# A third summed pair in the gate and up projections of an encoder block

## The chip, the cores and the metric

The kernel runs on one core of a Trainium2 chip. The metric is the device time of one execution in microseconds (us). One core has a matrix engine (TensorE, PE in the profile; its weight loads are listed as PEld), VectorE (DVE), ScalarE (ACT), GpSimd (POOL) and SyncE (SP, which here only issues DMAs). TensorE writes to PSUM, the other engines read PSUM and SBUF. All engines run side by side and wait for each other by semaphores; each takes its own instructions strictly in the order of its own list.

## The reference

One encoder layer over 256 tokens of width 2048, all in fp32: attention in two kinds of heads, cross-attention into 256 memory tokens, and a gated feed-forward network, each with a residual, and a last normalization. The change touches the feed-forward network:

```
hf = rms_norm(x, g_ffn)                                    # 256 x 2048
x  = x + (silu(hf @ w_gate) * (hf @ w_up)) @ w_down        # w_gate, w_up: 2048 x 5632, w_down: 5632 x 2048
out = rms_norm(x, g_final)
```

with `silu(z) = z * sigmoid(z)`.

## The kernel before

**Precision.** Every fp32 operand of a product is split into a high part (a cast to the reduced fp32r format) and a low part (what the cast left over). `split_into` (line 97) does it: ScalarE casts (line 99), VectorE subtracts (line 100). `mm` (line 89) then issues three matmuls: high x high (line 91), high x low (92), low x high (93). So each block product is three matmuls of 128 x 128 stationary by 128 x 512 moving columns. The activations are the stationary side and are split once; the weights are the moving side, come from HBM as fp32, are used once per core, and have to be split on the way.

**The weight path.** SyncE issues a DMA of 1 MB into one of three raw tiles (`wraw`, 128 x 2048). ScalarE and VectorE split it, 1024 columns at a time, into pairs of tiles `wh`, `wl`, a ring of four. Raw tile, ring tile and PSUM bank are each given out again when their last reader is done, so a DMA waits for VectorE, a cast waits for PE, and PE waits for VectorE.

**Wide projections.** The feed-forward network handles 512 hidden columns in a narrow first chunk (`narrow_chunk`, line 799) and 1024 in each of five wide chunks (`wide_chunk`, line 817). A wide chunk is a gate projection, an up projection (both `wide_result`, line 729), the product with the activation function, and the transposition of the result for the down projection (`wide_add`, line 749). All three go through `wide_project` (line 680). Its unit is a *pair*: two blocks of 128 along the contracted dimension, two token blocks, two blocks of 512 output columns. A pair of kind P, plain, is 2 x 2 x 2 = 8 block products, 24 matmuls. A pair of kind W uses sums of blocks (the Winograd form of Strassen's scheme): 7 block products, 21 matmuls. For that, the activations are kept as eight sums and blocks (`summed_pair`, line 663), and the weights are summed on VectorE before they are split (lines 707, 711 and 712). Three of the four output blocks share intermediate products, which collect in four PSUM banks `q1`, `q5`, `q7`, `q6` over all W pairs of a projection; after the last W pair, `leave` (line 733) takes them out with one copy on ScalarE and four operations on VectorE. The plain parts collect in four other banks, and `join` (line 742) adds the two at the end of the projection.

`GU_KINDS` (line 39) gives the kinds of the eight pairs of a gate or up projection: two of eight are W. The weights are laid out in HBM by these kinds. Within a W pair, seven blocks of weights are needed: three raw ones and four sums. Before, three split tiles of the ring take the raw blocks and two of the sums, and the other two sums go into a tile pair of their own (`wh2`, `wl2`).

**The activation function.** After a gate projection ScalarE computes a sigmoid of the four result blocks (line 824) and VectorE multiplies it with the result (line 825). The narrow chunk does the same with a scale (lines 808, 809).

**What sets the order.** The order of DMA issues is the program's (`keep_in_program_order`). The order of each engine's other instructions is set by the framework's planner, which runs the program against its own estimate of times and takes what is ready; so splits for a later pair stand between the matmuls and the joins of an earlier one. `pacc` and `pps` hold four PSUM banks each: the plain sums of the next projection can begin only when the joins have emptied the banks of the last.

Of the kernel before, what the change touches and what calls it, by code (L numbers as in the profile page):

```python
# [19 lines left out]
P = 128  # L20
S = 256
# [17 lines left out]
GU_KINDS = "PPWPWPPP"  # L39
# [35 lines left out]
def encoder_block(ctx: ExitStack, tc: tile.TileContext, a, out):  # L75
# [3 lines left out]
    wp = ctx.enter_context(tc.tile_pool(name="wp", bufs=3))  # L79
# [4 lines left out]
    pps = ctx.enter_context(tc.tile_pool(name="pps", bufs=4, space=PS))  # L84
    tables = ExitStack()
# [26 lines left out]

    def weights(src, fine=False, pool=None, before_k=None, cut=None, raw=None):
# [6 lines left out]
        if not begun:  # L120
            raw = wp.tile([P, 2048], F32, name="wraw", tag="wraw", bufs=3)
# [10 lines left out]
        for k in range(0, nk, step):  # L132
            n = min(step, nk - k)
            if pool:
                w = pool((P, n, ncols), "w")
            else:
                w = [wp.tile([P, 1024], F32R, name=x, tag=x, bufs=4)[:, :n * ncols].rearrange("p (k c) -> p k c", k=n)
                     for x in ("wh", "wl")]
                w = Split(*w)
# [26 lines left out]
    def nat(name):  # L166
        return sb.tile([P, 512], F32, name=name, tag="nat", bufs=7)
# [19 lines left out]
    lat_raw = wp.tile([P, 2048], F32, name="wraw", tag="wraw", bufs=3)  # L187
# [14 lines left out]
    posi = const.tile([P, NT], I32, name="posi")  # L202
    invf = const.tile([P, NF], F32, name="invf")
# [62 lines left out]
    posf = const.tile([P, NT], F32, name="posf")  # L266
# [81 lines left out]
    cosr = const.tile([P, NT, 2, DR // 2], F32, name="cosr")  # L348
    sinr = const.tile([P, NT, 2, DR // 2], F32, name="sinr")
    cosd = const.tile([P, NT, 2, DD // 2], F32, name="cosd")  # L350
    sind = const.tile([P, NT, 2, DD // 2], F32, name="sind")
# [155 lines left out]
    gdb = const.tile([P, DV], F32, name="gdb")  # L507
# [126 lines left out]
    wsum = ctx.enter_context(tc.tile_pool(name="wsum", bufs=1))  # L634


    def pair_raw(src):
        raw = wp.tile([P, 2048], F32, name="wraw", tag="wraw", bufs=3)
        raw = raw.rearrange("p (b c) -> p b c", b=4)
        tc.keep_in_program_order(nc.sync.dma_start(out=raw, in_=src))  # L640
        return raw

    def w_tile(n=2, pool=None):

        pool, tags, bufs = (wp, ("wh", "wl"), 4) if pool is None else (pool, ("wh2", "wl2"), 1)
# [3 lines left out]
    def split_blocks(src, pool=None):  # L649
        w = w_tile(src.shape[1], pool)  # L650
        split_into(w, src)
        return w
# [353 lines left out]
```

## Time and profile before

| what | value |
|---|---|
| time, median of 3 runs | 1158.89 us (1158.38 to 1160.23) |
| the profiled execution's own time | 1158.9 us |
| its span, first to last instruction | 1157.1 us |
| granted TensorE clock, mean | 0.999 |
| busy: PE, DVE, ACT, POOL | 99%, 78%, 53%, 6% of the span |
| matmuls and transposes | 5510 |
| DMA | 222.13 MB, 192 GB/s on average |

Busy times are sums over the span; an engine that is busy is not always the one that others wait for. In the groups of instructions, a line gives engine, operation, output and inputs, shapes and count, then the busy time of all, the mean of one in nanoseconds, and the idle time of that engine just ahead of them with the releaser. In the waits, the three numbers are the time in all, how often, and the longest. In the timeline, a line gives the start, the time from the first start to the last end of the merged instructions, and what they are. Matmul ends are modelled, so the distance from start to start is what to read there. In the windows, each engine's busy time stands with the number of its instructions.

### The profile page before, as it was taken

To read this page: it belongs to the slowest core of one execution; us is meant where nothing else is said; L and a number is where in the kernel's file an instruction comes from. 1 tells how busy PE (TensorE), PEld (TensorE's weight loads), DVE (VectorE), ACT (ScalarE), POOL (GpSimd) and SP (SyncE) were. 2 spreads that over 40 slices of the span, in tenths; PEclk is the share of its full clock that TensorE was granted. 3 is DMA by queue.
4 is the path that set the end of the run, shared out by engine and by line. 5 is a ranking of instruction groups with operands and counts; after the bars stand their busy time and mean duration, and the time that the engine had idled before them with its cause. 6 is when DMAs were issued, how large, how long until landed. Compare 5 with 4: busy or idle time off the path is not lost.

```text
span 1157.1 us, 14401 instructions
## 1 busy us (share of the span) xinstructions
PE 1148.1 (99%) x5510; PEld 961.7 (83%) x5510; DVE 901.3 (78%) x1197; ACT 611.0 (53%) x863; POOL 69.3 (6%) x81
## 2 busy tenths in 40 slices
PE   9999999999999999999999999999999999999997
PEld 7888888888888888888888888888888888888887
DVE  7698766586867776978888787797888788798873
ACT  6755454554665565655444554564544554554552
POOL 4920000001000000000000000000000000000021
PEclk9999999999999999999999999999999999999999
DMA  9565344435755445465565555645556555555651
GB/s 356 215 218 189 113 145 168 161 146 206 272 212 182 146 149 187 174 218 182 185 214 184 206 184 192 218 181 183 202 179 223 204 181 202 192 220 202 210 204 73
DMA packets 33764, 222.13 MB, mean 192 GB/s; under 512 B 4128, under 2 KB 4896, under 8 KB 8992
## 3 DMA queue, kind: packets, MB, share of 16 engines
q1 hardware_dynamic: 32256, 216.86, 52.4%
q0 software_dynamic: 864, 3.15, 0.7%
q10 hardware_dynamic: 576, 1.21, 0.3%
q8 instruction: 43, 0.70, 0.2%
q14 instruction: 25, 0.20, 0.1%
HBM read 219.11 MB, written 2.10 MB: 191 GB/s over the span
## 4 chain that ended last, share of the span: by engine, by line
PE 98%; DMA 1%; issue 0%; DVE 0%; SPq 0%; ACT 0%; POOLq 0%; POOL 0%; DVEq 0%; ACTq 0%
PE acc L92 28%; PE acc L91 28%; PE acc L93 28%; PE q L91 2%; PE q L92 2%; PE q L93 2%; PE pt L315 2%; PE ppt L462 1%; DMA wraw<-in_w_in_lat 1%; PE psc L93 1%; PE psc L91 1%; PE psc L92 1%; PE pt L838 0%; PE acckv L93 0%; PE acckv L92 0%
## 5 line engine op out<-in xcount | busy, mean ns | idle before, releaser
L99 ACT CAST wh<-wraw 128x1024 fp32r<-128x1024 f32 (+2 forms) x399 | 399.2, 1013 | 383.1 <-PE acc L93 346.7
L100 DVE TENSOR_TENSOR wl<-wraw,wh 128x1024 fp32r<-128x1024 f32 (+2 forms) x399 | 469.0, 1184 | 166.3 <-ACT wh L99 164.4
L92 PE MATMUL acc<-wl,x2n_h 128*128 128x512 f32 x480 | 185.5, 390 | 0.0
L93 PE MATMUL acc<-wh,x2n_l 128*128 128x512 f32 x480 | 185.2, 389 | 0.0
L91 PE MATMUL acc<-wh,x2n_h 128*128 128x512 f32 x480 | 160.3, 390 | 0.0
L93 PEld LDWEIGHTS acc<-wh,x2n_l 128*128 128x128 f32 x480 | 90.1, 188 | 18.8
L91 PEld LDWEIGHTS acc<-wh,x2n_h 128*128 128x128 f32 x480 | 90.1, 188 | 18.8
L92 PEld LDWEIGHTS acc<-wl,x2n_h 128*128 128x128 f32 x480 | 90.1, 188 | 18.7
L92 PE MATMUL acc<-wl,hT_h 128*128 128x512 f32 (+1 forms) x272 | 103.7, 381 | 0.0
L93 PE MATMUL acc<-wh,hT_l 128*128 128x512 f32 (+1 forms) x272 | 103.5, 381 | 0.0
L91 PE MATMUL acc<-wh,hT_h 128*128 128x512 f32 (+1 forms) x272 | 89.4, 382 | 0.0
L92 PE MATMUL acc<-wl,x0T_h 128*128 128x512 f32 x224 | 88.2, 395 | 0.0
L93 PE MATMUL acc<-wh,x0T_l 128*128 128x512 f32 x224 | 87.8, 393 | 0.0
L91 PE MATMUL acc<-wh,x0T_h 128*128 128x512 f32 x224 | 87.4, 396 | 0.3 <-ACT x0T_h L102 0.3
L99 ACT CAST wh<-tsum 128x1024 fp32r<-128x1024 f32 x56 | 58.3, 1047 | 42.2 <-DVE tsum L712 30.8
L100 DVE TENSOR_TENSOR wl<-tsum,wh 128x1024 fp32r<-128x1024 f32 x56 | 67.9, 1218 | 9.2 <-ACT wh L99 9.1
L91 PEld LDWEIGHTS acc<-wh,hT_h 128*128 128x128 f32 x272 | 51.2, 188 | 9.9 <-issue 0.2
L93 PEld LDWEIGHTS acc<-wh,hT_l 128*128 128x128 f32 x272 | 51.2, 188 | 9.6
L92 PEld LDWEIGHTS acc<-wl,hT_h 128*128 128x128 f32 x272 | 51.2, 188 | 9.4
L91 PEld LDWEIGHTS acc<-wh,x0T_h 128*128 128x128 f32 x224 | 42.2, 189 | 9.2 <-ACT x0T_h L102 1.2
L92 PEld LDWEIGHTS acc<-wl,x0T_h 128*128 128x128 f32 x224 | 42.3, 189 | 7.9 <-DVE wl L100 0.4
L93 PEld LDWEIGHTS acc<-wh,x0T_l 128*128 128x128 f32 x224 | 42.2, 188 | 7.6
(363 smaller groups left out, 2005.9 us busy)
## 6 DMA issues: line engine op xcount, KB each, us to landing
wraw<-in_w_gu SPq DMA_DIRECT2D x80, 1024.0 KB, 4.8
wraw<-in_w_dn SPq DMA_DIRECT2D x36, 1024.0 KB, 4.8
wraw<-in_w_in SPq DMA_DIRECT2D x24, 1024.0 KB, 4.8
wraw<-in_w_out SPq DMA_DIRECT2D x16, 1024.0 KB, 4.8
wraw<-in_w_down SPq DMA_DIRECT2D x8, 1024.0 KB, 4.8
wraw<-in_w_in_lat SPq DMA_DIRECT2D x7, 832.0 KB, 7.8
wraw<-in_w_xk SPq DMA_DIRECT2D x4, 1024.0 KB, 6.1
wraw<-in_w_xq SPq DMA_DIRECT2D x4, 1024.0 KB, 4.8
```

Source lines behind the costliest of these rows:

```text
L91: nc.tensor.matmul(o, l.h, r.h, start=start, stop=False)
L92: nc.tensor.matmul(o, l.h, r.l, start=False, stop=False)
L93: nc.tensor.matmul(o, l.l, r.h, start=False, stop=stop)
L99: last_cast[0] = nc.scalar.copy(out=dst.h, in_=src).ins
L100: last_split[0] = nc.vector.tensor_tensor(out=dst.l, in0=src, in1=dst.h.bitcast(F32), op=ALU.subtract).ins
L315: nc.tensor.transpose(out=pt[:, j * P:(j + 1) * P], in_=src[:, j * P:(j + 1) * P], identity=ident)
L462: nc.tensor.transpose(out=pt[:, kt * S + tt * P:kt * S + (tt + 1) * P], in_=p[:, tt, kt * P:(kt + 1) * P], identity=ident)
```

## The change

1. Pair 5 of each gate and up projection becomes W: three of eight instead of two, in gate and up of all five wide chunks. The order of the pairs becomes 0 to 7 in gate and 0, 2, 1, 4, 3, 5, 6, 7 in up (pairs 2, 4 and 5 are W). With five plain pairs, the last one's activations go into tiles of their own.
2. The split tiles of a W pair all come from the ring: the raw tile's first block is overwritten with a sum, so two split tiles take the raw tile and two take the other three sums. The additions are four of 512 instead of one of 1024 and two of 512. The order of the seven products changes a little. This holds for the down projection's W pairs too.
3. The ring grows from four split tiles to six at the end of the attention part, where a pool of tiles that only the attention part needs (`early`) is closed and a pool `late` takes its place. Its two tiles, the sums and five working tiles lie there. The raw ring stays at three.
4. Silu is one ScalarE function, written in place; the VectorE multiplications go.

```diff
-GU_KINDS = "PPWPWPPP"
+GU_KINDS = "PPWPWWPP"
...
+    class Ring:
+        def __init__(self, name, cols, dtype):
+            self.name, self.cols, self.dtype, self.slots, self.made = name, cols, dtype, [], 0
+        def more(self, pool, n):
+            self.slots = [(pool, f"{self.name}{self.made + i}") for i in range(n)] + self.slots
+            self.made += n
+        def next(self, name=None):
+            self.slots.append(self.slots.pop(0))
+            pool, tag = self.slots[-1]
+            return pool.tile([P, self.cols], self.dtype, name=name or self.name, tag=tag, bufs=1)
+
+    w_raw, w_high, w_low = Ring("wraw", 2048, F32), Ring("wh", 1024, F32R), Ring("wl", 1024, F32R)
+    w_raw.more(wp, 3)
+    w_high.more(wp, 4)
+    w_low.more(wp, 4)
+    nat_pool = [early, 7]
+    def split_tile(n, ncols):
+        return Split(*[ring.next()[:, :n * ncols].rearrange("p (k c) -> p k c", k=n) for ring in (w_high, w_low)])
...
     soft_pool.close()
-    wsum = ctx.enter_context(tc.tile_pool(name="wsum", bufs=1))
+    attention.close()
+    late = ctx.enter_context(tc.tile_pool(name="late", bufs=1))
+    nat_pool[:] = late, 5
+    w_high.more(late, 2)
+    w_low.more(late, 2)
+    def split_blocks(x):
+        blocks = []
+        for i in range(0, x.shape[1], 2):
+            n = min(2, x.shape[1] - i)
+            w = split_tile(n, 512)
+            split_into(w, x[:, i:i + n, :])
+            blocks += [w[:, j, :] for j in range(n)]
+        return blocks
...
-            t = wsum.tile([P, 4, 512], F32, name="tsum", tag="tsum", bufs=1)
-            b11 = split_blocks(raw[:, 1:3, :])
-            nc.vector.tensor_tensor(out=t[:, 0:2, :], in0=raw[:, 1:3, :],
-                                    in1=raw[:, 0:1, :].to_broadcast([P, 2, 512]), op=ALU.add)
-            t13 = split_blocks(t[:, 0:2, :])
-            b21 = split_blocks(raw[:, 3:4, :])
-            nc.vector.tensor_tensor(out=t[:, 2, :], in0=t[:, 0, :], in1=raw[:, 2, :], op=ALU.add)
-            nc.vector.tensor_tensor(out=t[:, 3, :], in0=t[:, 2, :], in1=raw[:, 3, :], op=ALU.add)
-            t24 = split_blocks(t[:, 2:4, :], wsum)
+            t = late.tile([P, 3, 512], F32, name="tsum", tag="tsum", bufs=1)
+            for o, x, y in ((t[:, 0, :], raw[:, 0, :], raw[:, 2, :]), (raw[:, 0, :], raw[:, 0, :], raw[:, 1, :])):
+                nc.vector.tensor_tensor(out=o, in0=x, in1=y, op=ALU.add)
+            t1, b11, b22, b21 = split_blocks(raw)
+            for o, x, y in ((t[:, 1, :], raw[:, 0, :], raw[:, 2, :]), (t[:, 2, :], t[:, 1, :], raw[:, 3, :])):
+                nc.vector.tensor_tensor(out=o, in0=x, in1=y, op=ALU.add)
+            t3, t2, t4 = split_blocks(t)
...
-            mm(Q[1], A11, b11[:, 0, :], *own)
-            mm(accs[0][1], S3, b11[:, 1, :], False, stop)
-            mm(Q[5], S5, t13[:, 0, :], *own)
-            mm(Q[7], S7, t13[:, 1, :], *own)
-            mm(accs[0][0], A12, b21[:, 0, :], False, stop)
-            mm(Q[6], S6, t24[:, 0, :], *own)
-            mm(accs[1][0], A22, t24[:, 1, :], False, stop)
+            mm(Q[1], A11, b11, *own)
+            mm(Q[5], S5, t1, *own)
+            mm(accs[0][1], S3, b22, False, stop)
+            mm(accs[0][0], A12, b21, False, stop)
+            mm(Q[7], S7, t3, *own)
+            mm(Q[6], S6, t2, *own)
+            mm(accs[1][0], A22, t4, False, stop)
...
-                if n == 4:
+                if n == 4 and "P" in GU_KINDS[i + 1:]:
                     t, n = act_tile(name="x2n"), 0
+                elif n == 4:
+                    t = Split(*[late.tile([P, 2, S], F32R, name="odd" + x, tag="odd" + x, bufs=1) for x in "hl"])
+                    n = 0
...
-            nc.scalar.activation(sg, ga[tt], AF.Sigmoid, scale=r)
-            nc.vector.scalar_tensor_tensor(out=sg, in0=ga[tt], scalar=r, in1=sg, op0=ALU.mult, op1=ALU.mult)
+            nc.scalar.activation(sg, ga[tt], AF.Silu, scale=r)
...
-    GU_SEQ = list(range(len(GU_KINDS)))
+    GATE_SEQ, UP_SEQ = (0, 1, 2, 3, 4, 5, 6, 7), (0, 2, 1, 4, 3, 5, 6, 7)
...
-        g = wide_result(xn, a["w_gu"][c, 0], GU_SEQ)
+        g = wide_result(xn, a["w_gu"][c, 0], GATE_SEQ)
         for tt in range(NT):
             for oc in range(2):
-                sg = nat("sg")
-                gs = g[tt][:, oc, :]
-                nc.scalar.activation(sg, gs, AF.Sigmoid)
-                nc.vector.tensor_tensor(out=gs, in0=gs, in1=sg, op=ALU.mult)
-        u = wide_result(xn, a["w_gu"][c, 1], GU_SEQ)
+                nc.scalar.activation(g[tt][:, oc, :], g[tt][:, oc, :], AF.Silu)
+        u = wide_result(xn, a["w_gu"][c, 1], UP_SEQ)
```

More of the change, by code (lines that the diff above doesn't have):

```diff
@@ L120, in weights @@
         if not begun:
-            raw = wp.tile([P, 2048], F32, name="wraw", tag="wraw", bufs=3)
+            raw = w_raw.next()
         raw = raw[:, :nk * ncols].rearrange("p (k c) -> p k c", k=nk)
@@ L186, in encoder_block @@
     LAT = KVL + DR
-    lat_raw = wp.tile([P, 2048], F32, name="wraw", tag="wraw", bufs=3)
+    lat_raw = w_raw.next()
     for c0, c1 in ((0, QL), (QL, QL + LAT)):
```

50 lines of the change are left out of this document (18 added, 32 removed).

## The prediction

> **What bounds the kernel now.** I read the page first: its busy shares and the chain of work that ended last.
>
> ```profile
> span 1157.1 us, 14401 instructions
> PE 1148.1 (99%) x5510; PEld 961.7 (83%) x5510; DVE 901.3 (78%) x1197; ACT 611.0 (53%) x863; POOL 69.3 (6%) x81
> ...
> PE 98%; DMA 1%; issue 0%; DVE 0%; SPq 0%; ACT 0%; POOLq 0%; POOL 0%; DVEq 0%; ACTq 0%
> ```
>
> TensorE fills the span. A busy PE need not be a PE at its pace, so the second view is the timeline of PE, for the distance from one matmul to the next, first in a stretch of plain pairs and then across a summed pair.
>
> ```profile
> 642.66 0.40 PE L91 MATMUL acc<-wh,forms_h 128*128 128x512 f32 x1
> 642.90 0.40 PE L91 MATMUL q<-wh,forms_h 128*128 128x512 f32 x1
> ...
> 647.52 1.07 PE L91 MATMUL acc<-wh,x2n_h 128*128 128x512 f32 x4
> ...
> 657.82 1.07 PE L91 MATMUL acc<-wh,x2n_h 128*128 128x512 f32 x4
> ...
> 660.54 1.07 PE L91 MATMUL acc<-wh,x2n_h 128*128 128x512 f32 x4
> ```
>
> From 657.82 to 660.54 lie 12 matmuls of 512 columns (half a plain pair): 0.2267 us each, with nothing between them. A plain pair of 24 is 5.44 us. From 642.66 to 647.52 lie the 21 matmuls of a summed pair: 4.86 us, 0.2314 each, so its matmuls come a little slower. The chain gives the same over a longer way, from one place in the gate projection of chunk 1 to the same place in its up projection:
>
> ```profile
> 669.54 0.45 PE acc L91 x2
> ...
> 711.87 0.45 PE acc L91 x2
> ```
>
> 42.33 us for six plain pairs and two summed ones. Six times 5.44 is 32.64, which leaves 4.85 us for a summed pair. So in the ten wide gate and up projections time is the number of matmuls times a constant pace.
>
> Who supplies PE, and with how much room? Third view, the waits (the second row is from those of SyncE's queue), and then the windows of chunk 4 and of the end of the narrow chunk.
>
> ```profile
> ACT wh L99 <- PE acc L93: 358.0, 220, 7.1
> ...
> DVE wl L100 <- ACT wh L99: 173.5, 156, 3.6
> ```
>
> ```profile
> SPq L640 <- DVE wl L100: 575.2, 115, 9.7
> ```
>
> ```profile
> core 0: us, PE busy (x) PEld busy (x) DVE busy (x) ACT busy (x) POOL busy (x), PEclk, DMA share, GB/s
> ...
> 460.00:488.00 28.00, 28.00 (x127) 23.20 (x126) 27.70 (x41) 16.89 (x25) 0.00 (x0) 1.00 0.48 168
> ...
> 974.00:1018.00 44.00, 44.00 (x203) 36.41 (x202) 36.26 (x48) 23.79 (x31) 0.00 (x0) 1.00 0.51 182
> 1018.00:1062.00 44.00, 44.00 (x195) 36.33 (x194) 37.17 (x43) 23.23 (x26) 1.10 (x2) 1.00 0.61 222
> ```
>
> The reader is to see the direction of the waits: the cast that makes `wh` waits for PE to give a ring tile back (220 times), VectorE's subtraction waits for the cast, and SyncE waits for VectorE to free a raw tile. The supply is ahead of PE and is held back by places to put its work. But VectorE is 82 to 84% busy there, and this change gives it more.
>
> **The change part by part.**
>
> *A sixth kind becomes W.* Pair 5 of each of the ten wide projections needs 21 matmuls where it needed 24. Value: 5.44 - 4.85 = 0.59 us, times ten is 5.9 us off PE. Bounds: if the three matmuls go at the pace of the plain ones, 3 x 0.2267 x 10 = 6.8; if all 21 keep the slower pace seen at 642.66 (the next start there, at 642.90, is 0.24 later), 5.44 - 21 x 0.234 = 0.53, so 5.3.
>
> *What it adds to VectorE.* Durations and distances:
>
> ```profile
> L100 DVE TENSOR_TENSOR wl<-wraw,wh 128x1024 fp32r<-128x1024 f32 x354 | 432.0, 1228 | 152.4 <-ACT wh L99 150.5
> ...
> L707 DVE TENSOR_TENSOR tsum<-wraw 128x1024 f32<-128x1024 f32 x28 | 34.1, 1218 | 2.9 <-DMA wraw<-in_w_dn 2.2 <-DMA wraw<-in_w_gu 0.2
> ...
> L711 DVE TENSOR_TENSOR tsum<-tsum,wraw 128x512 f32<-128x512 f32 x28 | 19.1, 683 | 0.1
> ...
> L825 DVE TENSOR_TENSOR res<-res,sg 128x512 f32<-128x512 f32 x20 | 13.1, 681 | 0.0
> ```
>
> ```profile
> 659.73 2.35 DVE L100 TENSOR_TENSOR wl<-wraw,wh 128x1024 fp32r<-128x1024 f32 x2
> ...
> 672.26 1.28 DVE L744 TENSOR_TENSOR res<-acc,res 128x512 f32<-128x512 f32 x2
> ```
>
> Two of 1024 take 2.35, so the second starts 1.13 behind the first; two of 512 take 1.28, a step of 0.60. I count steps, 1.14 and 0.60. A plain pair is two subtractions, 2.28. A summed pair was one addition of 1024, two of 512, three subtractions of 1024 and one of 512: 4 x 1.14 + 3 x 0.60 = 6.36. Now it is four additions of 512, three subtractions of 1024 and one of 512: 3.42 + 3.00 = 6.42. Each projection therefore gets 6.42 - 2.28 = 4.14 for pair 5 and 2 x 0.06 for the old two: 4.26 us.
>
> The Trainium skill, page "VectorE: DVE Perf Modes", section "The DRAIN you can't avoid", says that a VectorE operation starts only when the pipe behind the one before has emptied, though one that is not held starts sooner. By the first half the full 1.23 and 0.68 count and VectorE would be over its limit, the third rival below. The 2.35 us for two in the row above follow the second half.
>
> *What silu takes from it.* Four multiplications at line 825 in each gate projection go: 4 x 0.60 = 2.4. ScalarE runs four activations as before, with another function:
>
> ```profile
> L99 ACT CAST wh<-wraw 128x1024 fp32r<-128x1024 f32 x354 | 368.4, 1052 | 353.3 <-PE acc L93 322.9 <-issue 10.3 <-PE q L93 4.9
> ...
> L99 ACT CAST wh<-wraw 128x512 fp32r<-128x512 f32 x29 | 18.0, 620 | 24.7 <-PE acc L93 23.8 <-DMA wraw<-in_w_in_lat 0.9
> ...
> L824 ACT ACTIVATE sg<-res 128x512 f32<-128x512 f32 x20 | 12.2, 627 | 9.1 <-DVE res L744 9.0
> ...
> L808 ACT ACT_TABLE_LOAD x1 | 1.3, 1283 | 0.0
> ```
>
> So the fullest gate stage goes from 36.26 to 36.26 + 4.26 - 2.4 = 38.1 of VectorE in 44.0 - 0.6 = 43.4 us of PE (88%); the up stage from 37.17 to 41.4 in 43.4 (95%). ScalarE gets 3 x 1.05 + 0.62 - 2 x 1.05 = 1.7 per projection, to some 25 of 43. Both lie beside PE; I cost them at nothing as long as the lead holds. What hides them is the ring: six tiles ahead of PE, of which a plain pair takes two and a summed one four, against four plus one. When PE begins pair 0 of a gate projection, pairs 0 and 1 are split and pair 2 is begun. The work left by the up projection behind it (joins, products, splits of `hT`, the forms) and the rest of pair 2 have two pairs, 10.9 us, and the transposes. If the cover is gone, every us by which VectorE is late in a stage is a us of PE, five times over the chunks.
>
> *The order of the summed pairs.* In gate pairs 4 and 5 follow each other: 2 x 6.42 = 12.8 us of VectorE against 2 x 4.85 = 9.7 of PE. 3.1 us must come from the lead, which plain pair 3 ahead of them builds (5.44 of PE, 2.28 of VectorE: 3.2). It just covers. In up they alternate, 8.7 of VectorE to 10.3 of PE. I take nothing, bounds 0 and 3.1 x 5.
>
> *Raw tiles and DMA.* As many transfers; three raw tiles as before; a raw tile is let go after its last addition or split, as now.
>
> ```profile
> wraw<-in_w_gu SPq DMA_DIRECT2D x80, 1024.0 KB, 4.8
> ```
>
> 4.8 us to land with three in rotation and a pair every 5.2 us: 2.4 us of VectorE idling at line 707 came from a DMA in the whole run. Nothing, and at most that 2.4 again.
>
> *Third summed form of the activations.* Once, in the narrow chunk: four operations of 128 elements and 512 more elements split, at most 5 x 0.60 = 3.0 us of VectorE by the step for 512. It falls into the window 460 to 488, where VectorE is busy for 27.70 of 28.00 and PE still for all 28.00. Two products of 512 (line 809) leave the same window, at least 1.2. Nothing, bounds -1.2 and 1.8. The other edits (pools opened and closed, `nat` tiles, names) issue no instruction.
>
> *Sum.* The profiled execution took 1158.9 us with a span of 1157.1 and 1.8 around it; the median of the runs is 1158.89, the same. 1158.9 - 5.9 = 1153.0; I say 1152.9, from 0.595 x 10 unrounded. Own range 1151.6 to 1154.4: the bounds 6.8 and 5.3 (1152.1 to 1153.6), each moved by half a us or more for the spread of the runs.
>
> **The rivals.**
>
> 1. *VectorE becomes the bound in the up stage* (the slower side). It idles 44.00 - 37.17 = 6.83 us there now. With 41.4 to do in 43.4, it may keep 2.0 of these. If half stay (3.4), it is 1.4 late, times five 7: 1160. If three quarters stay (5.1), 3.1 late, 15.7: 1168.6. Slower from about 3.9 kept. For it: the idle time stands behind casts, and with more additions ahead of each cast there are more such steps. Against it: those casts wait for PE's tiles, so the idle time is that of a supply that is ahead, and in the window 460 to 488 VectorE had 0.3 us left and PE lost nothing.
>
> 2. *Pair 5 right behind pair 4 in gate comes late.* Without the lead of pair 3, 3.1 us five times is 15; half of it, 7.7: 1160.7. Against it: two more ring tiles than before at just this place.
>
> 3. *Held VectorE operations.* The up stage would have 43 + 8 instructions, each 0.085 longer than its step (1.228 against 1.14, 0.683 against 0.60): 4.3 on top of 41.4 is 45.7, 2.3 late, times five 11.5: 1164.4. This is the rule named above; the pairs of instructions shown speak against it.
>
> 4. *Silu needs a table that the casts do not share.* The profile has one load, at line 808, and none between sigmoids and casts, though they take turns:
>
> ```profile
> 672.98 0.63 ACT L824 ACTIVATE sg<-res 128x512 f32<-128x512 f32 x1 [3.03 <-DVE res L744]
> 673.70 1.05 ACT L99 CAST wh<-wraw 128x1024 fp32r<-128x1024 f32 x1
> 674.66 0.62 ACT L824 ACTIVATE sg<-res 128x512 f32<-128x512 f32 x1
> 675.19 1.04 ACT L99 CAST wh<-wraw 128x1024 fp32r<-128x1024 f32 x1
> 676.12 1.15 ACT L824 ACTIVATE sg<-res 128x512 f32<-128x512 f32 x2
> ```
>
> If silu's table lacked the copy, these three runs of activations would cost six loads of 1.28, 7.7 us of ScalarE per gate, inside the lead of 10.9: up to a few us, 1153 to 1158. The Trainium skill, page "ScalarE: Activation LUTs", section "Table sets: the hidden batching unit", says that cheap functions such as copy are in every set, which would rule this out; no run shows it yet for silu. By that page's 2.66 us for a switch, six switches would be 16 us a gate, and the time about 1178.
>
> **How the numbers follow.** Forecast 0.66. Rival 1: 0.25, of which 0.07 eats under 3.7 us (still faster), 0.08 lands near 1160, 0.10 near 1168. Rival 2: 0.05, near 1160. Rival 3: 0.02. Rival 4: 0.02, counted slower. A measurement of this kernel tells 0.2%, 2.3 us, from no change: faster is below 1156.6, slower above 1161.2. So faster 0.66 + 0.07 = 0.73, same 0.08 + 0.05 = 0.13, slower 0.10 + 0.02 + 0.02 = 0.14. The range from 1150.8 (below 1151.6, should the summed pairs' slower pace go too: 0.1 us for each of the old ones) to 1161.5 takes in the forecast and the cases near 1160 and leaves out about 0.14.
>
> **What would show it.** Right: the same place of gate and up lies 41.7 us apart (5 x 5.44 + 3 x 4.85), 30 fewer matmuls, VectorE near 38 and 41 us in the stages of chunk 4, one table load at silu, and no wait of PE beyond 0.3 us there. Rival 1: PE waits for `wl` in the up stages and VectorE's waits for ScalarE stay above 2 us a stage. Rival 2: PE waits at pair 5 of gate alone. Rival 3: VectorE's instructions no longer overlap. Rival 4: more than four table loads. A span of 1157 with 30 fewer matmuls would prove the forecast wrong.

## The result and the profile after

The changed kernel takes 1175.12 us (median of 4 runs, 1174.38 to 1176.0) against 1159.18 us for the kernel before beside it (4 runs): a ratio of 1.0136, 95% interval 1.0122 to 1.0149. It is 1.4% slower. The prediction said 1152.9 us, faster, with 1161.5 as its upper end and a chance of 0.14 for slower. It was wrong in sign.

The page of the kernel after, with the rows that answer to those shown of before:

```profile
span 1174.1 us, 14413 instructions
...
PE 1154.7 (98%) x5480; PEld 958.3 (82%) x5480; DVE 930.3 (79%) x1269; ACT 626.0 (53%) x885; POOL 66.5 (6%) x81
...
PE 94%; DVE 2%; DMA 2%; ACT 1%; issue 1%; POOLq 0%; POOL 0%; DVEq 0%; ACTq 0%
```

The 30 matmuls are gone (5510 to 5480), and yet PE is busy for 6.6 us more than before, while its share of the chain fell from 98% to 94%. So there are two losses: PE waits, and PE's instructions themselves come more slowly. The windows show where it waits. The columns are the length of the window, each engine's busy time with its count of instructions, the granted clock, the share of the DMA engines and the rate. The first three rows are gate, up and the down projection's part of chunk 2, the last one that of chunk 4:

```profile
core 0: us, PE busy (x) PEld busy (x) DVE busy (x) ACT busy (x) POOL busy (x), PEclk, DMA share, GB/s
718.50:766.80 48.30, 46.16 (x207) 36.76 (x206) 40.41 (x56) 23.77 (x32) 0.00 (x0) 1.00 0.43 159
766.80:807.80 41.00, 41.00 (x180) 33.61 (x179) 38.75 (x46) 24.69 (x28) 0.00 (x0) 1.00 0.64 227
807.80:858.70 50.90, 48.45 (x211) 39.05 (x210) 40.48 (x55) 22.45 (x30) 0.00 (x0) 0.97 0.46 169
...
1074.20:1126.30 52.10, 49.55 (x217) 39.96 (x216) 41.43 (x54) 25.12 (x36) 2.24 (x2) 0.97 0.45 167
```

In up, PE is busy for all 41.00 us; in gate and in the down projection's part 2.1 to 2.6 us are missing, and in the latter the clock is below 1 as well. PE's timeline of gate in chunk 2 shows both losses:

```profile
736.08 0.39 PE L93 MATMUL acc<-wh,x2n_h 128*128 128x512 f32 x1
...
738.58 0.39 PE L95 MATMUL acc<-wh,x2n_l 128*128 128x512 f32 x1
...
742.24 0.39 PE L93 MATMUL q<-wh,forms_h 128*128 128x512 f32 x1
...
743.64 0.63 PE L93 MATMUL acc<-wh,forms_h 128*128 128x512 f32 x2
...
746.21 0.50 PE L94 MATMUL q<-wl,forms_h 128*128 128x512 f32 x1 [0.53 <-DVE wl L102]
...
748.54 0.97 PE L93 MATMUL acc<-wh,x2n_h 128*128 128x512 f32 x3 [1.14 <-ACT wh L101]
749.99 0.73 PE L93 MATMUL q<-wh,forms_h 128*128 128x512 f32 x2 [0.48 <-ACT wh L101]
```

The *stops* stand at 746.21, 748.54 and 749.99, where PE waits for a split tile. The *slow steps* are quieter: from 736.08 to 738.58 eleven matmuls start 2.50 us apart, 0.2273 each; from 742.24 to 743.64 six take 1.40, 0.2333 each, and nothing is waited for.

I sorted every distance between the starts of two matmuls from 484 us on (the feed-forward network) in this way: what lies over 0.3 us counts as a stop, with its excess over 0.227; what lies between 0.22 and 0.3, for 512 columns, counts as slow with its excess over 0.2267. Matmuls at half clock come 0.43 apart and so count as stops.

| kernel | matmuls and transposes | stops, us | slow steps, us |
|---|---|---|---|
| before | 5510 | 1.2 | 2.9 |
| after | 5480 | 17.7 | 9.4 |

30 matmuls at 0.2267 are 6.8 us less, the stops 16.4 more, the slow steps 6.5 more: 16.1 in all. The runs show 15.9. (The profiled executions, 1176.0 and 1158.9, lie 17.1 apart; the other 1.0 us lies ahead of 484 us.) Two theories follow, one for each term.

**Theory B, for the stops.** The four PSUM banks `q1`, `q5`, `q7`, `q6` of the next projection are those that the transposes of the last result have used. In the compiled program `q6` and `q7` of gate in chunk 2 lie in the banks that the last two transposed tiles filled from 726.73 and from 728.33 on. VectorE reads these two late (the sums and splits of the `forms`). The planner therefore puts the products into `q7` and `q6` of the first W pair far back in PE's list, behind other pairs. Their split tile stays in use until then. The ring gives its tiles out in turn, so a later split has to wait for exactly this tile although others are free. Here are the rows of VectorE's timeline in that gate stage:

```profile
737.71 0.94 DVE L102 TENSOR_TENSOR forms_l<-pt,forms_h 128x256 fp32r<-128x256 f32 x2
...
740.13 1.23 DVE L102 TENSOR_TENSOR wl<-wraw,wh 128x1024 fp32r<-128x1024 f32 x1 [0.69 <-ACT wh L101]
743.56 1.23 DVE L102 TENSOR_TENSOR wl<-wraw,wh 128x1024 fp32r<-128x1024 f32 x1 [2.21 <-ACT wh L101]
744.93 1.23 DVE L102 TENSOR_TENSOR wl<-tsum,wh 128x1024 fp32r<-128x1024 f32 x1
...
747.44 0.68 DVE L731 TENSOR_TENSOR tsum<-wraw 128x512 f32<-128x512 f32 x1
```

and of ScalarE's, and of the waits of SyncE's queue in 715 to 760:

```profile
742.48 1.05 ACT L101 CAST wh<-wraw 128x1024 fp32r<-128x1024 f32 x1 [2.39 <-PE acc L95]
743.84 1.05 ACT L101 CAST wh<-tsum 128x1024 fp32r<-128x1024 f32 x1 [0.31 <-PE q L95]
```

```profile
SPq L717 <- DVE tsum L734: 22.9, 2, 15.0
```

The last transposes of the result end at 728.9; the last to read them, the split of the forms from `pt`, is done at 738.65. The products of pair 2 into `q7` and `q6` run from 742.24 to 743.64, behind pair 3 and a part of pair 4. Right behind them, at 743.84, ScalarE casts the sums of pair 4 into the tile that they held. In the compiled program the same tile then goes to the first half of pair 6, cast at 747.44: the stops at 746.21 and 748.54 are both of this one tile. The one buffer for sums is free only after the subtraction that begins at 744.93, and one more subtraction follows it, so pair 5's first addition begins at 747.44; its raw tile is let go late, and SyncE's queue, whose transfers keep the program's order, waits up to 15.0 us. Meanwhile ScalarE idles 2.39 and VectorE 2.21 us, just ahead of a stop that is theirs. No row names the bank: PE never waits for it, since the order was written with the wait in it.

In the down projection's part the same ends in a transfer that comes too late (the chain of waits from 835 to 849 us):

```profile
835.71 1.06 ACT wh L101
836.80 1.24 DVE wl L102
838.05 4.83 DMA wraw<-in_w_dn
...
842.99 1.06 ACT wh L101
...
844.07 2.36 DVE wl L102 x2
```

The cast at 835.71 follows the release of a held tile; the raw tile is free at 838.05, the transfer takes 4.83, and PE has to wait for the cast and the subtraction behind it:

```profile
846.46 1.20 PE L93 MATMUL acc<-wh,hT_h 128*128 128x512 f32 x4 [1.29 <-ACT wh L101]
848.82 0.80 PE L94 MATMUL acc<-wl,hT_h 128*128 128x512 f32 x1 [1.15 <-DVE wl L102]
```

One stop of the kernel after is of another kind. At the end of up in chunk 3 VectorE waits 2.19 us for a transfer with an addition that stands ahead of the joins in its list, and PE waits for a join (VectorE's row, then PE's):

```profile
980.49 0.69 DVE L731 TENSOR_TENSOR tsum<-wraw 128x512 f32<-128x512 f32 x1 [2.19 <-DMA wraw<-in_w_gu]
```

```profile
983.07 0.47 PE L93 MATMUL acc<-wh,x2n_h 128*128 128x512 f32 x1 [0.93 <-DVE res L766]
```

**Theory A, for the slow steps.** In the compiled program the two new split tiles lie in the pool `late`, with other remainders on division by 512 bytes than the four old ones and the activations. In the kernel after, sorted by where the moving tile and the stationary tile of the *next* matmul lie (whose load runs meanwhile), the mean steps from 484 us on are 0.2282 for old split tile and old activation (1639 of them), 0.2336 for new split tile and old activation (822), 0.2338 for old split tile and the new activation tiles `odd` (146), and 0.2285 where both lie in `late` (95). So it is not the new place, but the pair. In its first form the theory asked for multiples of 64 bytes, which `late` misses; the second form, equal remainders modulo 512, was made after the first round.

### The profile page after: what moved, and what is told of

Its sections match the earlier page's. It is cut to its first block, busy times and chain, and to the rows that moved or that the text cites. A ratio compares the mean times of both kernels' runs of the same rounds, so it can differ in the third digit from the quotient of the medians.

```text
span 1174.1 us, 14413 instructions
## 1 busy us (share of the span) xinstructions
PE 1154.7 (98%) x5480; PEld 958.3 (82%) x5480; DVE 930.3 (79%) x1269; ACT 626.0 (53%) x885; POOL 66.5 (6%) x81
## 4 chain that ended last, share of the span: by engine, by line
PE 94%; DVE 2%; DMA 2%; ACT 1%; issue 1%; POOLq 0%; POOL 0%; DVEq 0%; ACTq 0%
PE acc L94 26%; PE acc L95 26%; PE acc L93 26%; PE q L93 3%; PE q L94 3%; PE q L95 3%; PE pt L340 2%; DVE wl L102 1%; ACT wh L101 1%; DMA wraw<-in_w_gu 1%; PE ppt L487 1%; PE psc L95 1%; PE psc L94 1%; PE psc L93 1%; PE acckv L93 0%
## 5 line engine op out<-in xcount | busy, mean ns | idle before, releaser
L94 PE MATMUL acc<-wl,x2n_h 128*128 128x512 f32 x320 | 125.5, 393 | 0.0
L95 PE MATMUL acc<-wh,x2n_l 128*128 128x512 f32 x320 | 125.2, 393 | 0.0
L93 PE MATMUL acc<-wh,x2n_h 128*128 128x512 f32 x320 | 114.7, 394 | 3.2 <-ACT wh L101 2.3
L101 ACT CAST wh<-tsum 128x1024 fp32r<-128x1024 f32 (+1 forms) x76 | 61.8, 834 | 40.1 <-PE acc L95 21.7
L102 DVE TENSOR_TENSOR wl<-tsum,wh 128x1024 fp32r<-128x1024 f32 (+1 forms) x76 | 70.2, 951 | 16.5 <-ACT wh L101 16.1
L93 PEld LDWEIGHTS acc<-wh,x2n_h 128*128 128x128 f32 x320 | 59.9, 188 | 17.6 <-ACT wh L101 3.1
L95 PEld LDWEIGHTS acc<-wh,x2n_l 128*128 128x128 f32 x320 | 60.1, 188 | 13.3
L94 PEld LDWEIGHTS acc<-wl,hT_h 128*128 128x128 f32 x272 | 52.2, 192 | 13.6 <-DVE wl L102 3.2
L94 PE MATMUL q<-wl,forms_h 128*128 128x512 f32 x152 | 59.8, 394 | 1.1 <-DVE wl L102 1.1
L95 PEld LDWEIGHTS acc<-wh,hT_l 128*128 128x128 f32 x272 | 52.0, 191 | 10.5
L95 PE MATMUL q<-wh,forms_l 128*128 128x512 f32 x152 | 59.4, 392 | 0.0
L93 PE MATMUL q<-wh,forms_h 128*128 128x512 f32 x152 | 49.9, 395 | 0.9 <-ACT wh L101 0.9
```

Source lines behind the costliest of these rows:

```text
L93: nc.tensor.matmul(o, l.h, r.h, start=start, stop=False)
L94: nc.tensor.matmul(o, l.h, r.l, start=False, stop=False)
L95: nc.tensor.matmul(o, l.l, r.h, start=False, stop=stop)
L101: last_cast[0] = nc.scalar.copy(out=dst.h, in_=src).ins
L102: last_split[0] = nc.vector.tensor_tensor(out=dst.l, in0=src, in1=dst.h.bitcast(F32), op=ALU.subtract).ins
```

## The experiments

All times are medians; ratios are to the kernel before on the same chip. From 484 us on the traces gave:

| run | us | ratio, 95% interval | stops | slow steps |
|---|---|---|---|---|
| e1, `late` at a multiple of 64 bytes | 1174.02 | 1.0126 (1.0111 to 1.0141) | 15.5 | 8.7 |
| e3, two split tiles for sums alone | 1159.75 | 1.0003 (0.9994 to 1.0013) | 4.2 | 6.9 |
| e4, two W of eight | 1165.49 | 1.0054 (1.0037 to 1.0071) | 1.9 | 8.6 |
| e5, gate in the order of up | 1172.72 | 1.0119 (1.0104 to 1.0134) | 13.6 | 9.8 |
| e6, banks free early | 1160.06 | 1.0010 (1.0000 to 1.0019) | 3.1 | 9.5 |
| e7, addresses equal modulo 512 | 1163.91 | 1.0043 (1.0026 to 1.0060) | 15.5 | 0.8 |
| e8, e3 with e6 and e7 | 1150.27 | 0.9924 (0.9909 to 0.9939) | 1.8 | 0.4 |
| e9, e8 with two W | 1156.69 | 0.9982 (0.9972 to 0.9991) | 2.2 | 0.4 |
| e10, e8 with sigmoid and product | 1151.61 | 0.9936 (0.9921 to 0.9951) | 3.1 | 0.7 |
| e11, before with equal addresses | 1156.18 | 0.9977 (0.9967 to 0.9987) | 1.3 | 0.4 |
| e12, e8 with `late` 256 bytes on | 1150.66 | 0.9928 (0.9913 to 0.9943) | 1.8 | 0.5 |
| e13, e6 with e7 | 1150.54 | 0.9927 (0.9913 to 0.9942) | 2.3 | 0.7 |

**First round: one suspected cause at a time.** A pad moves `late` to a multiple of 64 bytes:

```diff
+    nc.gpsimd.memset(small.tile([P, 8], F32, name="pad", bufs=1), 0.0)
```

> The changed kernel with one tile of 32 bytes more ahead of the pool `late`, so that its tiles begin on a multiple of 64 bytes, as the tiles of the other pools do (in the compiled program of the changed kernel they are 32 bytes off). Nothing else moves. Theory A (a matmul whose moving tile and whose next stationary tile lie differently within 64 bytes takes 0.233 instead of 0.227 us): the matmuls with a step between 0.230 and 0.240 all but vanish outside the stops, 6 us less, about 1169; the stops of PE in the gate stages of chunks 2 and 4 and in the first down projection behind them stay, some 16 us. Rival: it is the place high in SBUF, or PE catching up with its supply: no change, 1175.

1.1 us of 15.9 instead of the expected 6, and the slow steps went from 9.4 to 8.7. Theory A in this form falls.

The sums of a W pair get two split tiles of their own, the rest keeps four:

```diff
-    w_high.more(late, 2)
-    w_low.more(late, 2)
+    s_high, s_low = Ring("sh", 1024, F32R), Ring("sl", 1024, F32R)
+    s_high.more(late, 2)
+    s_low.more(late, 2)
...
-            t3, t2, t4 = split_blocks(t)
+            t3, t2, t4 = split_blocks(t, (s_high, s_low))
```

> The changed kernel with the same number of split tiles, but two of the six set aside for the two split tiles of a summed pair that hold sums (t3, t2 and t4); the other four make the ring. Theory B (the stops come from a ring tile that is pinned: the products into q7 and q6 wait for PSUM banks that the transposes of the chunk before still hold, and their split tile blocks the ring for the pairs behind): the stops fall from 16 us to under 4, and as plain pairs no longer use tiles of `late`, some 3 to 4 us of slow steps go too: 1156 to 1161. Rival 1 of the prediction (VectorE has too much to do): the same work, so no change, 1173 to 1177.

15.4 us are gained with not one instruction of work fewer. The stops fell from 17.7 to 4.2; the slow steps fell by 2.5, since plain pairs no longer use tiles of `late`. A ring in which a held tile doesn't stand in front of the others is what was missing, and VectorE, just as loaded (930.3 us in the kernel after), keeps up:

```profile
PE 1145.6 (99%) x5480; PEld 956.0 (83%) x5480; DVE 934.7 (81%) x1269; ACT 624.6 (54%) x885; POOL 68.7 (6%) x81
```

The third summed pair is undone, the rest of the change is kept:

```diff
-GU_KINDS = "PPWPWWPP"
+GU_KINDS = "PPWPWPPP"
```

> The changed kernel with the old kinds, PPWPWPPP: no third summed pair; the ring of six, the new order of sums and products, and silu stay. Theory B: the stops in the down projections behind chunks 2 and 4, some 9 us, stay, since these have the same pairs as before; the stops in the gate stages, some 7 us, go, since no pair 5 comes right behind pair 4; 30 matmuls more, 6.8 us: 1172 to 1178. Rival 1 (VectorE's work): with the old load all stops go: 1159 plus 6 for the slow steps, 1163 to 1166.

Here the stops all but went (1.9), those of the down projection's part too. Theory B as I first put it had not expected this; 1165.49 lies in the range that rival 1 had given. So the stops need the third pair as well as the ring; whether by its work on VectorE, by its sums in the ring or by its shorter time on PE this run doesn't separate. The first fits what the traces have for the first down-projection part of chunk 2, from the transposes into the bank of `q6` to the end of VectorE's last read of the forms: 10.5 us before, 13.2 after, 10.9 here. With 10.9 the held tile seems to come back in time. What is left here over the kernel before, 6.3 us, is the slow steps (5.7).

Gate takes its pairs in the order of up, so that pairs 4 and 5 no longer follow each other:

```diff
-    GATE_SEQ, UP_SEQ = (0, 1, 2, 3, 4, 5, 6, 7), (0, 2, 1, 4, 3, 5, 6, 7)
+    GATE_SEQ, UP_SEQ = (0, 2, 1, 4, 3, 5, 6, 7), (0, 2, 1, 4, 3, 5, 6, 7)
```

> The changed kernel with gate in the order of up (0, 2, 1, 4, 3, 5, 6, 7), so that no two summed pairs follow each other. Rival 2 of the prediction (pair 5 right behind pair 4 is late): the stops in the gate stages go, 6 to 7 us: about 1168. Theory B: pair 2 comes one pair earlier and its q7 and q6 wait longer for their banks; the stops stay or grow: 1175 to 1182.

2.4 us of 15.9, between what the two theories expected. The stops in gate of chunk 2 fell from 3.0 to 1.1 us, with 0.5 more at the start of up, those in the down projection's part only from 4.6 to 4.0. In gate of chunk 2 the neighbours make more than half of the stops; they are not the cause of the rest.

**Second round: both theories by their causes.** ScalarE copies the upper half of the last two transposed tiles out, and the last summed pair is made from the copy:

```diff
                 pts.append(pt.rearrange("p (j t) -> p j t", t=P))
+                if tt == 0:
+                    pc = nat("pc").rearrange("p (n t) -> p n t", n=4)
+                nc.scalar.copy(out=pc[:, 2 * tt:2 * tt + 2, :], in_=pts[tt][:, 2:4, :])
...
-                summed_pair(pts[0][:, 2:4, :], pts[1][:, 2:4, :], True)]
+                summed_pair(pc[:, 0:2, :], pc[:, 2:4, :])]
```

> The kernel after, with one edit: ScalarE copies the upper half of each token block's last two transposed PSUM tiles of silu(gate) x up into SBUF, and the last summed pair is added from that copy, so those two PSUM banks need not wait for VectorE's last sums and splits of the hand-over. Everything else, the ring of six with its six W kinds among it, is as in the kernel after. Theory B (the matmuls of the next stage's pairs 2 and 3 wait for these banks, keep their split tiles in the ring, and so hold back the casts behind them): the stops of PE from 484 us on, 17.7 us in the kernel after, fall under 5 us, the slow steps of 0.2335 us stay at about 9 us, and the time is 1161 to 1165 us. If the banks are not what holds the ring (the splits of the forms themselves, or ScalarE, are late): the stops stay above 12 us and the time is 1171 to 1177 us; ScalarE's two added copies per token block could add up to 2 us.

The stops fell to 3.1, with the slow steps where they were; 15.1 us are gained. The same gate stage, ScalarE's rows and then PE's:

```profile
728.87 0.37 ACT L864 COPY pc<-pt 128x256 f32<-128x256 f32 x1 [0.59 <-PE pt L860]
729.14 0.38 ACT L101 CAST hT_h<-pt 128x256 fp32r<-128x256 f32 x1
```

```profile
734.44 0.40 PE L95 MATMUL q<-wh,forms_l 128*128 128x512 f32 x1
734.67 1.09 PE L93 MATMUL acc<-wh,x2n_h 128*128 128x512 f32 x4
```

The copies have read the upper halves by 729.24, and the lower halves are split right behind. The products into `q7` and `q6` now follow at once on the others of their pair and end at 734.67, 9.0 us earlier than in the kernel after. SyncE's longest wait for the sums fell from 15.0 to 7.9 us; their total (22.9 before this edit) did not, which points to the one late issue:

```profile
SPq L717 <- DVE tsum L734: 22.7, 3, 7.9
```

Theory B holds. What this run doesn't separate is the copy itself from the earlier place that the planner gave the sums because of it. A second buffer for the sums, the one that holds pair 5 back in the trace above, wasn't tried; what it would be worth is not shown.

Five small tiles move from one pool to another, so that the addresses of all split tiles and activations leave the same remainder on division by 512 (one of the five shown):

```diff
-    first = small.tile([P, 1], F32, name="first", bufs=1)
+    first = const.tile([P, 1], F32, name="first")
```

> The kernel after, with five small tiles (a few hundred bytes per partition) moved from one pool to another, so that the split tiles of the last pool lie at addresses that leave the same remainder on division by 512 bytes as those of the other split tiles and of the activations. No instruction is added or removed. Theory A, second form (the matmul step is 0.2335 instead of 0.2275 us where the moving tile and the stationary tile of the next matmul differ in address modulo 512 bytes): the slow steps, 9.4 us in the kernel after, fall under 2 us and the time is 1166 to 1169 us, the stops being untouched. Rival (the step depends on how high in SBUF the tile lies, or on the pair of regions, whatever the alignment): the slow steps stay at 8 to 9.5 us and the time is 1174 to 1176 us.

11.2 us, more than expected: the slow steps fell from 9.4 to 0.8 and the stops by 2.2. The six products that took 1.40 us in the kernel after, in this run:

```profile
737.88 0.39 PE L93 MATMUL q<-wh,forms_h 128*128 128x512 f32 x1
...
739.24 0.61 PE L93 MATMUL acc<-wh,forms_h 128*128 128x512 f32 x2
...
741.81 0.50 PE L94 MATMUL q<-wl,forms_h 128*128 128x512 f32 x1 [0.54 <-DVE wl L102]
...
744.14 0.97 PE L93 MATMUL acc<-wh,x2n_h 128*128 128x512 f32 x3 [1.13 <-ACT wh L101]
```

1.36 us for the same six, 0.2267 each, from the same tiles in `late`; the stops behind them stand as before. In the compiled programs every engine has the same instructions in the same order as in the kernel after, so the addresses alone did this: Theory A in its second form holds. The two losses are nearly independent. The 2.2 us of stops that went are in the main the single stop at the end of up in chunk 3 and a half-clock stretch in chunk 2 that didn't come.

All three edits on the kernel after:

> Three edits at once on the kernel after: two of the six split tiles set apart for the summed pairs and four left for the rest, the PSUM halves copied out early by ScalarE, and the addresses made equal modulo 512 bytes. If Theory B and Theory A in its second form both hold, the stops fall to 1.5 to 4 us and the slow steps under 2 us: 1151 to 1155 us, below the kernel before. If only Theory B holds (the slow steps stay): 1157 to 1160 us. If neither adds to what the two reserved tiles gave: 1159 to 1161 us.

1150.27 us, 24.9 below the kernel after and 0.76% faster than the kernel before. The stops and slow steps are down to 2.2 us together. Then the same with two W pairs of eight:

> The same as the run with all three edits, but gate and up with only two of their eight K pairs as block sums (PPWPWPPP), so 30 matmuls more. This prices the third summed pair where nothing stops: by the matmuls alone it is worth 10 times 0.59 us, so this run is 5 to 7 us longer than the run with all three edits. If the third summed pair costs VectorE more than PE gains even with the ring relieved, the two runs are within 1 us of each other or this one is shorter.

6.4 us more: the third summed pair is worth 0.64 us for each of the ten projections, once nothing stands in its way.

**Third round: what is left.** Silu as before the change, on e8 (the same edit once more, with its scale, in the narrow chunk):

```diff
-                nc.scalar.activation(g[tt][:, oc, :], g[tt][:, oc, :], AF.Silu)
+                sg = nat("sg")
+                gs = g[tt][:, oc, :]
+                nc.scalar.activation(sg, gs, AF.Sigmoid)
+                nc.vector.tensor_tensor(out=gs, in0=gs, in1=sg, op=ALU.mult)
```

> The run with all three edits (two reserved split tiles, banks copied out early, equal addresses modulo 512 bytes; 1150.3 us), with silu as before the change: ScalarE's sigmoid and one more product on VectorE for each, 20 of 128x512 in gate and 4 in the other part. This prices silu. If the lead of the ring covers it, as the prediction costed it: 1150 to 1151.5 us. Rival (VectorE, busy 933 of 1148 us, is the last to be ready behind each gate): 2.4 us for each of up to five gates show in part, 1153 to 1160 us.

1151.61 (1151.25 to 1151.67) against 1150.54 (1150.25 to 1150.82) for e13 beside it. The runs don't overlap, but e13 also differs from e10 in the ring. Against e8, on another chip, it is 1.3 us, with the stops up from 1.8 to 3.1; against e12 beside it 0.95, with runs that overlap (1149.86 to 1151.33). So silu is worth about 1 us, and not more closely known. That lies between what the two theories expected, nearer to a covered gain.

The kernel before the change with e7's edit:

> The kernel before the change, with the same five small tiles moved so that the addresses of its sixth pair of split tiles are equal modulo 512 bytes to the others'; no instruction added or removed. Theory A, second form: the kernel before has 168 slow steps of the summed pairs and their spill, 2.9 us from 484 us on; the time falls to 1156 to 1157.5 us. Rival (the slow steps come from the change's code alone, or alignment helps only where six tiles rotate): no change, 1158.5 to 1160 us.

2.7 us faster with no instruction changed, as expected. The kernel before had slow steps too, on the sums that had tiles of their own.

A pad moves `late` by 256 bytes on e8:

```diff
+    nc.gpsimd.memset(small.tile([P, 64], F32, name="pad", bufs=1), 0.0)
```

> The run with all three edits (1150.3 us), with the last pool moved by 256 bytes, so that its split tiles differ from the other tiles by 256 modulo 512 bytes (differences of 160, 192, 320 and 352 were slow, 0 was fast). If all of the 512 bytes count, about 580 matmul steps are 0.233 again and some neighbours with them: 1154 to 1157 us. If only the remainder modulo 256 counts: 1150 to 1151 us.

No slow steps: 0.2267 for 583 matmuls whose tiles differ by 256. So the remainder modulo 256 counts, or that modulo 128: the slow differences seen were 160, 192, 320 and 352, none of them a multiple of 128, and a difference of 128 wasn't tried.

The last run leaves the ring of six as it was in the kernel after and has the other two edits:

> The kernel after with two of the three edits: the banks copied out early and the equal addresses; the ring of six is left as in the kernel after, with no tile set apart for the sums. If the two gains add (15.1 us for the banks, 11.2 us for the addresses, of which the addresses gave 8.6 us in slow steps and the rest in stops that the banks take anyway): 1150.5 to 1152.5 us, and setting tiles apart is worth nothing once the banks are free. If the ring still has to be relieved: 1153 to 1158 us.

1150.54, the same as e8 within the spread: once the banks are free, no tile needs to be set apart. Of the 24.6 us between the kernel after and this one, 15.4 are stops and 8.7 slow steps.

## Why the prediction was wrong

*"A sixth kind becomes W", 5.9 us: right.* e9 less e8 is 6.4, inside the bounds 5.3 to 6.8 and near the upper one, since in e8 and e9 all matmuls keep the pace of 0.2267. In the stretch where the kernel after doesn't stop, the gain can be seen: from the first join of gate to the last join of up in chunk 1 (the joins' groups, with the first and the last start), before, after and e13:

```profile
L744 DVE TENSOR_TENSOR res<-acc,res x8: 679/682/685, 672.3 to 718.2; 128x512 f32<-128x512 f32 x8
```

```profile
L766 DVE TENSOR_TENSOR res<-acc,res x8: 677/680/682, 672.9 to 718.5; 128x512 f32<-128x512 f32 x8
```

```profile
L766 DVE TENSOR_TENSOR res<-acc,res x8: 680/684/686, 669.1 to 714.3; 128x512 f32<-128x512 f32 x8
```

45.9, 45.6 and 45.2 us. Predicted was 0.6 less than before; after has 0.3, the rest is slow steps; e13 has 0.7.

*"What it adds to VectorE": right.* Ten times 4.26, less 12 for silu and 1.2 in the narrow chunk, is 29.4, without the third form (at most 3.0); the page shows 930.3 against 901.3, 29.0. The steps kept overlapping (the two subtractions at 844.07 take 2.36 us), so rival 3, held operations, is out.

*"I cost them at nothing as long as the lead holds": this step failed.* The lead was counted in free tiles, "six tiles ahead of PE, of which a plain pair takes two and a summed one four". But the ring gives tiles out in turn, and the lead ends at the oldest tile that is still held. How long each of a W pair's tiles is held, from the split to its last product, I didn't ask; for the sums into `q7` and `q6` that hangs on PSUM banks, which I had not listed as a resource of the change at all, though I named the work that is late ("the splits of `hT`, the forms") in the same sentence. Before the change the forms were as late in gate of chunk 2 (12.2 us by the measure used for e4, 11.9 after). But there the product into `q6` read from a split tile of its own (`wh2`), outside the ring; the change put all sums into the one ring. The product into `q7` held a tile of the ring before as well, up to the matmul at 740.60, and PE didn't stop: that tile went next to a plain pair that PE began to read only at 744.02, where the tile in the kernel after went to the sums of pair 4, read from 745.02, and then to pair 6. So a late product alone doesn't stop PE; it does when the next in turn is needed soon. e3 gives the sums tiles of their own again, and 13.5 us of stops go.

The sum had no term for the down projection either, though the change takes its W pairs in too. About half of the stops of the kernel after lie there, and before the change VectorE was fuller there than in any gate or up stage:

```profile
804.00:846.00 42.00, 42.00 (x194) 34.75 (x193) 38.32 (x51) 21.40 (x28) 0.00 (x0) 1.00 0.55 198
```

*"The order of the summed pairs", nothing, at most 15.5: nearly right.* 2.4 us by e5, inside the bounds; rival 2 alone would have given 7.7 for half.

*"Pools opened and closed, `nat` tiles, names issue no instruction": this step failed too.* They issue none, but they move tiles, and where the tiles lie cost 6.5 us more than before. The trace of before showed it: the matmuls at 642.66 and 642.90, quoted there, lie 0.24 apart, and the first of them reads `wh2`. I put the slower pace down to summed pairs and priced it for the new pairs only. The right question would have been which tile those matmuls read, and the answer, a tile outside the first pool, would have covered a third of all split tiles in the change. e4, with two W and 8.6 us of slow steps, shows that it isn't the number of summed pairs.

*"What silu takes", beside PE: nearly right.* 1 us of the 12 that VectorE saves shows (e10 against e13).

*Raw tiles and DMA, nothing: wrong as a consequence.* No transfer got slower (4.83 us from issue to landing at 838.05, against 4.8), but one is issued up to 15.0 us late where its raw tile is held by the ring. In e6 the longest is 7.9 and PE doesn't feel it.

*Rival 1, VectorE as the bound in up (1160 to 1168.6), had the right sign, but the wrong place and too little.* In up of chunk 2 PE is busy for 41.00 of 41.00 us; the stops lie in the stages behind a transposition, but for the one of 0.93 us at the end of up in chunk 3. Its half truth is e4, which ended in the range that it gave: with less work on VectorE the forms come earlier and the stops go. Yet e6 and e13 do all the work of three W pairs and hardly stop, and in e13's gate and up of chunk 4 PE has no gap. VectorE's 41.68 and 36.80 us there are 78.5 in sum, near the 38.1 and 41.4 of the prediction (79.5); more of it lies in gate. (A slip beside this: the prediction has slower begin at about 3.9 us kept; by its own numbers it is 3.7.) The two windows:

```profile
969.00:1012.80 43.80, 43.80 (x203) 36.34 (x202) 41.68 (x58) 25.04 (x33) 0.00 (x0) 1.00 0.48 172
1012.80:1054.20 41.40, 41.40 (x185) 34.27 (x184) 36.80 (x44) 23.62 (x26) 1.10 (x2) 1.00 0.64 236
```

*Rival 4, a table that lacks the copy, is out.* The groups of ScalarE after show four loads in all, as before, of which one is in the narrow chunk, and none between silu and casts (the prediction's "one load" is that of the narrow chunk):

```profile
L847 ACT ACTIVATE res<-res 128x512 f32<-128x512 f32 x20 | 12.3, 629 | 11.1 <-DVE res L766 11.1
...
L833 ACT ACT_TABLE_LOAD x1 | 1.3, 1283 | 0.0
```

The Trainium skill, page "ScalarE: Activation LUTs", section "Table sets: the hidden batching unit", has the cheap functions such as copy in every set; this trace agrees.

Put together: the change without its two side effects is worth 1156.18 (e11, before with equal addresses) less 1150.54 (e13), 5.6 us, close to the 6.0 predicted. The side effects cost 24.6, of which the kernel before paid 2.7 too (e11).

## What to carry to other kernels

A ring given out in turn is as deep as its longest-held tile allows. Before putting more kinds of tiles into one ring, write down for each kind how long it is held and by what, PSUM banks included; a kind that may be held long gets tiles of its own, or what holds it is copied out early. Where an order is written ahead of time, such a hold is seen in no wait row: look for producers that idle just ahead of the stop they cause. And an edit that only moves tiles is not free: compare the steps of the same instruction by the tile that it reads.

## What the runs showed of the hardware

**The step of a matmul depends on where its moving tile and the next stationary tile lie relative to each other.** 0.2267 us for 128 x 512 where the two addresses differ by 256 modulo 512 bytes (e12), 0.2269 to 0.2270 where they are equal (e12, e7), 0.233 to 0.234 where they differ by 160, 192 or 352, 0.231 where by 320. Steps of equal remainders were slower in the kernel after as well: 0.2318 right behind such a pair (110 steps), and still 0.2279 where neither neighbour is one (1489). Why the latter are slow is not shown; in e7, where all are equal, they are not. The slow steps were 9.4 us of 1175 in the kernel after and 2.9 of 1159 before. The Trainium skill, page "TensorE: Matmul & The Clock Gate", section "Step-by-step: what each phase is for", says that TensorE reads the moving operand and the next weights through two independent ports, so that a load takes nothing from the running matmul. These runs differ: e7, which changes addresses alone, makes the matmuls 2.8% shorter where the remainders had differed (0.2336 to 0.2270). Why is not shown.

**The clock fell to half behind the stops of two stages out of four.** Behind the stops in the down projection's part of chunk 2, in steps of 2 us:

```profile
844.00:846.00 2.00, 1.17 (x6) 0.59 (x4) 1.93 (x2) 2.00 (x4) 0.00 (x0) 1.00 0.39 152
846.00:848.00 2.00, 1.20 (x4) 0.67 (x4) 2.00 (x4) 1.70 (x3) 0.00 (x0) 1.00 0.00 0
848.00:850.00 2.00, 1.19 (x3) 0.99 (x4) 2.00 (x4) 0.70 (x1) 0.00 (x0) 0.71 0.21 25
850.00:852.00 2.00, 2.00 (x7) 1.52 (x6) 2.00 (x2) 0.00 (x0) 0.00 (x0) 0.50 0.84 315
852.00:854.00 2.00, 2.00 (x10) 1.66 (x9) 2.00 (x5) 0.00 (x0) 0.00 (x0) 0.94 1.01 426
```

About 3.4 us at half clock (0.29 + 0.5 + 0.06 of 2 us lost, 1.7 us), after PE had idled 1.29 and 1.15 us and been busy for over half of the time. Behind gate's waits in the same chunk (0.53, 1.14 and 0.48 us) the clock stayed at 1.00. The Trainium skill, page "TensorE: Matmul & The Clock Gate", section "What's actually happening", has the clock fall after an idle window of about 3.4 us; the length of the half-clock stretch agrees with that figure, but here less idle time was enough, in pieces. So a part of what the stops cost (1.7 of 4.6 us at this place) is their echo in the clock. How much idle time it takes is not shown: in e7 stops of 1.36 and 1.15 us left the clock at 1.00 in chunk 2, and stops of 1.34 and 1.15 us took it to 0.50 in chunk 4:

```profile
844.00:846.00 2.00, 2.00 (x10) 1.67 (x9) 2.00 (x3) 0.00 (x0) 0.00 (x0) 1.00 0.79 266
```

```profile
1104.00:1106.00 2.00, 1.99 (x5) 1.60 (x6) 2.00 (x3) 0.00 (x0) 0.00 (x0) 0.50 0.52 98
```
